# Gathering 32-row blocks as two transfers of 64 partitions, and building their plain form on TensorE

## The chip, the cores and the metric

The kernel runs on one core of a Trainium2 chip. The metric is the device time of one execution in microseconds. TensorE is called PE below, ScalarE ACT, VectorE DVE, GpSimd POOL and SyncE SP; SP, POOL and ACT also issue DMA transfers.

## The reference

One inference step of a two-layer trunk, for a prompt of 512 tokens and for 8 samples of 4 tokens each, which share the weights. Layer 0 mixes tokens with a gated DeltaNet, layer 1 with sliding-window attention; a SwiGLU block follows each. The change lies in the DeltaNet. Cut to what matters, with 16 heads of width 128 (the kernel works in chunks of 128 rows, the reference in chunks of 64; the recurrence is the same):

```python
kb = k * beta[..., None]
Bm = where(strict, einsum('bhncd,bhnsd->bhncs', kb, k) * decay, 0.0)
M = -Bm
T = eye(C) + M                       # T becomes inverse(I + Bm)
for _ in range(1, ...):
    Mp = Mp @ Mp
    T = T + T @ Mp
u = einsum('bhncs,bhnse->bhnce', T, v * beta[..., None])
...
def step(S, xs):                     # over the chunks, in sequence
    unew = uc - einsum('bhcd,bhde->bhce', wc, S)
    o = einsum(..., qc * exp(Gc), S) + einsum(..., ac, unew)
    S = S * exp(Gl) + einsum('bhcd,bhce->bhde', kc * exp(Gl - Gc), unew)
```

Each head's triangular matrix I + Bm is inverted chunk by chunk, and the state S then runs through the chunks.

## The kernel before

The Tile framework orders the instructions; the program order that it starts from is a string, PLAN (line 37). The 16 heads are four groups of four heads, g = 0 to 3, and the sequence is four chunks of 128. The steps of a group:

- t (tphase, lines 598 to 772): Gram matrices and decays on PE, ACT and DVE give `ba`, the 128x128 triangular blocks of 4 heads and 4 chunks, in two halves of two chunks.
- The inverse of the sixteen 32x32 diagonal blocks of a head is made on POOL. The blocks are written to DRAM (tile D1, line 702) and gathered into Lb (line 720) with one block on each partition. There are 64 blocks; Lb holds them twice, on partitions 0 to 63 and 64 to 127, so that each copy solves 16 of the 32 columns. A loop of 31 steps (lines 727 to 733) subtracts products, two instructions a step: `subt` and `Tn`. DVE transposes the result into `Tt` (line 735).
- Both forms then go through DRAM (tile D2): Tn and Tt are written (lines 740 and 741); the plain form is read into TU (line 746), the transposed form into the diagonal blocks of `ba` (line 750).
- m (merge, lines 774 to 817): two rounds of small matmuls per half (`pw`, `py`, and again `pw` and `py` at 64x64) turn the 32x32 inverses into 128x128 ones.
- c (chain, lines 838 to 890): over the four chunks `pk`, `pq`, `pu` on PE, the copy `un` on ACT, then `pS` and the new S on DVE, and `po`.
- s (sample, from line 900): the same for the 8 samples; o (out, line 1014): normalise, transpose, gate.

Beside them run the projections as dense passes: `win` (q, k, v), `wz` (gate), and `wa`, `wb` (two of the three passes of w_out, `wo`). Each dense product is three matmuls, since operands are split in high and low parts; one line (159) issues them. They are what PE does while a group's steps wait. The operands of `wa` are loaded from DRAM by eight SP transfers (`ogl`, line 300).

Tiles are taken from rings by tag. `sub` has three buffers (Lb, Tn, the samples' `wk` and Ue); `un` and `Kd` have one each. In `un` live the chain's un, the samples' `up` and merge's W2, in `Kd` the chain's Kd and the samples' `kp`. An instruction that writes a new tile of a tag waits until the last reader of the old one is done. POOL, too, works in program order, and has other small work: copies around the convolution (lines 539 to 549), memsets, and the reciprocal roots `rk` and `ro` (line 214).

Of the kernel before, what the change touches and what calls it, by code (L numbers as in the profile page):

```python
# [9 lines left out]
F32 = mybir.dt.float32  # L10
# [5 lines left out]
P = 128  # L16
# [10 lines left out]
NCH = SEQ // P  # L27
# [48 lines left out]
def kernel(  # L76
# [178 lines left out]
    with ExitStack() as gctx:  # L255
# [40 lines left out]
        def w_out_first():  # L296
# [9 lines left out]
            w_out_pass(0, ops)  # L306

        ops, ss1 = gdn(gctx, tc, locals())
        w_out_pass(2, ops)

# [87 lines left out]
def gdn(ctx, tc, env):  # L398
    nc, PE, DVE, ACT, POOL = (env[k] for k in ("nc", "PE", "DVE", "ACT", "POOL"))
    tmp, bank, dense, halves = (env[k] for k in ("tmp", "bank", "dense", "halves"))  # L400
    pc, kc, ident, ones, hrhs, rsqrt_col = (env[k] for k in ("pc", "kc", "ident", "ones", "hrhs", "rsqrt_col"))
    fillers = env["fillers"]
    dpool, ogsc = env["dpool"], env["ogsc"]
# [21 lines left out]
    p2 = ctx.enter_context(tc.tile_pool(name="g2", bufs=2))  # L425

    def big(tag, name, bufs, dt=F32, rows=P):
        return p2.tile([rows, 1024], dt, tag=tag, name=name, bufs=bufs)
# [169 lines left out]
    def tphase(q):  # L598
        g, KQ, KQS = q.g, q.KQ, q.KQS
# [76 lines left out]
        D1 = dpool.tile([4, NCH, 4, 32, 32], F32, tag="D1", name=f"D1_{g}")  # L676
        for hf in range(2):
            ba = p2.tile([P, 2, 4, 2, P], F32, tag="BA", name=f"BA{g}_{hf}", bufs=4)
            q.BA.append(ba)
            for n2 in range(2):  # L680
                n = 2 * hf + n2
                gr = bank("t", f"gram{g}_{n}")
                for j in range(2):
                    PE.matmul(gr[:, j * 256:(j + 1) * 256], lhsT=KQ[j][:, n, 0, :],
                              rhs=KQ[j][:, n].rearrange("p a b -> p (a b)"), start=True, stop=True)
                for j in range(2):
                    pe = bank("t", f"pe{g}_{n}_{j}")
                    PE.matmul(pe, lhsT=sel[:, n:n + 1].to_broadcast([68, P]),
                              rhs=bd[:, 4 * j:4 * j + 4].rearrange("p a b -> p (a b)"), start=True, stop=False)
                    PE.matmul(pe.rearrange("p (i c) -> p i c", i=2), lhsT=identr,  # L690
                              rhs=maskp.unsqueeze(1).to_broadcast([P, 2, 256]), start=False, stop=True)
                    for i in range(2):
                        h = 2 * j + i
# [6 lines left out]
            for b in range(4):  # L700
                bs = slice(32 * b, 32 * b + 32)
# [7 lines left out]
                  start=True, stop=False)  # L709
# [7 lines left out]


        Lb = big("sub", f"Lb{g}", 3)
        nc.sync.dma_start(Lb, D1.rearrange("b n h s c -> (b n h) (s c)").unsqueeze(0).to_broadcast([2, 64, 1024]))  # L720
        Lb = Lb.rearrange("p (s c) -> p s c", s=32)
        TU = big("sub", f"Tn{g}", 3)
        Tn = TU[:, :512].rearrange("p (s c) -> p s c", s=32)
        POOL.memset(Tn, 0.0)
        for k in range(2):
            POOL.memset(TU[64 * k:64 * k + 64, 16 * k:512:33], 1.0)
        for j in range(31):
# [6 lines left out]
        Tt = Lb.rearrange("p s c -> p (s c)")[:, :512].rearrange("p (c s) -> p c s", s=32)  # L734
        DVE.tensor_copy(Tt, Tn.rearrange("p a b -> p b a"))

        D2 = dpool.tile([2, 4, NCH, 4, 32, 32], F32, tag="D2", name=f"D2_{g}")
        for k in range(2):
            ks = slice(64 * k, 64 * k + 64)
            nc.sync.dma_start(D2[0].rearrange("b n h s c -> (b n h) s c")[:, :, 16 * k:16 * k + 16], Tn[ks])  # L740
            nc.sync.dma_start(D2[1].rearrange("b n h (s k) c -> k (b n h) s c", k=2)[k], Tt[ks])
        TU = TU.rearrange("p (u c) -> p u c", c=64)
        POOL.memset(TU[0:32, :, 32:64], 0.0)
        for b in range(3):
            o = 32 if b == 1 else 0
            nc.sync.dma_start(TU[32 * b:32 * b + 32, :, o:o + 32], D2[0, b].rearrange("n h s c -> s (n h) c"))
        for hf in range(2):
            for b in range(4):
                bs = slice(32 * b, 32 * b + 32)
                nc.sync.dma_start(  # L750
                    q.BA[hf][bs, :, :, 0, bs].rearrange("p n h c -> p (n h) c"),
                    D2[1, b, 2 * hf:2 * hf + 2].rearrange("n h s c -> s (n h) c"),
                )


# [13 lines left out]
        DVE.tensor_tensor(MT, MT, ident, ALU.add)  # L769
        DVE.tensor_tensor(q.TTs, pm3[:, 0:P], MT, ALU.add)  # L770

        q.TU = TU

    def merge(q):

        g, TU = q.g, q.TU
        for hf in range(2):
            ba = q.BA[hf]
            us = [(n2, h, 8 * hf + 4 * n2 + h) for n2 in range(2) for h in range(4)]

            def plain(t):

                return t.rearrange("p (b k c) -> p b c k", k=2, c=16)

            W1 = p2.tile([P, 8, 32], F32, tag="E", name=f"W1{g}_{hf}", bufs=2)
            pw = bank("v", f"pw{g}_{hf}")
            for i, (n2, h, u_) in enumerate(us):
                c = slice(i * 32, i * 32 + 32)
                PE.matmul(pw[32:64, c], lhsT=ba[0:32, n2, h, 0, 32:64], rhs=plain(TU[0:32, u_, 0:32]), start=True, stop=True)
                PE.matmul(pw[96:128, c], lhsT=ba[64:96, n2, h, 0, 96:128], rhs=plain(TU[64:96, u_, 0:32]), start=True, stop=True)  # L790
            for r in (32, 96):
                ACT.mul(W1[r:r + 32].rearrange("p h c -> p (h c)"), pw[r:r + 32, 0:256], -1.0)
            py = bank("v", f"py{g}_{hf}")
            for i, (n2, h, u_) in enumerate(us):
                c = slice(i * 32, i * 32 + 32)
                PE.matmul(py[0:32, c], lhsT=W1[32:64, i, :], rhs=ba[32:64, n2, h, 0, 32:64], start=True, stop=True)
                PE.matmul(py[32:64, c], lhsT=ba[32:64, n2, h, 0, 32:64], rhs=W1[32:64, i, :], start=True, stop=True)
                PE.matmul(py[64:96, c], lhsT=W1[96:128, i, :], rhs=ba[96:128, n2, h, 0, 96:128], start=True, stop=True)

            def v8c(t):  # L800
                return t.rearrange("p (n h c) -> p n h c", n=2, h=4)

            ACT.copy(ba[0:32, :, :, 0, 32:64], v8c(py[0:32, 0:256]))
            ACT.copy(TU[32:64, 8 * hf:8 * hf + 8, 0:32].rearrange("p u (k c) -> p u c k", k=2),
                     py[32:64, 0:256].rearrange("p (u c k) -> p u c k", u=8, k=2))
            ACT.copy(ba[64:96, :, :, 0, 96:128], v8c(py[64:96, 0:256]))
            pw2 = bank("v", f"pw2{g}_{hf}")
            for i, (n2, h, u_) in enumerate(us):
                c = slice(i * 64, i * 64 + 64)
                PE.matmul(pw2[64:128, c], lhsT=ba[0:64, n2, h, 0, 64:128], rhs=plain(TU[0:64, u_, :]), start=True, stop=True)  # L810
            W2 = p2.tile([P, 8, 64], F32, tag="un", name=f"W2{g}_{hf}", bufs=1)
            ACT.mul(W2[64:128].rearrange("p h c -> p (h c)"), pw2[64:128, 0:512], -1.0)
            py2 = bank("v", f"py2{g}_{hf}")
            for i, (n2, h, u_) in enumerate(us):
                c = slice(i * 64, i * 64 + 64)
                PE.matmul(py2[0:64, c], lhsT=W2[64:128, i, :], rhs=ba[64:128, n2, h, 0, 64:128], start=True, stop=True)
            ACT.copy(ba[0:64, :, :, 0, 64:128], v8c(py2[0:64, 0:512]))
# [283 lines left out]


    steps = {"kq": proj_kq, "t": tphase, "v": proj_v, "p": states, "s": sample, "m": merge, "c": chain, "z": proj_z, "o": out}
    groups = {}
    for step in PLAN.split():
# [10 lines left out]
        else:  # L1116
            g = int(step[-1])
# [419 lines left out]
```

## Time and profile before

| | us |
|---|---|
| median of 3 runs | 1753.47 |
| lowest, highest | 1748.12, 1753.71 |
| profiled execution | 1754.97 |
| its span in the trace | 1753.2 |
| PE busy in the span | 1648.0 (94%) |
| DVE, ACT, POOL busy | 947.7, 754.0, 230.0 |

The profiled execution is 1.8 us longer than its span and 1.5 us above the median. The DeltaNet takes the stretch from the start to 721 us, where the first SwiGLU's `wg` begins; the last `wz` matmuls end at about 541 us. In rows of the trace the names are the program's without the buffer numbers: `D` is D1 or D2, `Tn` also TU. A busy PE row counts a matmul from start to modelled end, so lengths of neighbours overlap.

### The profile page before, as it was taken

What the parts mean: (1) busy time and instruction counts of PE and PEld (TensorE: products, weight loads), DVE (VectorE), ACT (ScalarE), POOL (GpSimd) and SP (SyncE); (2) the same over time, 40 slices, a digit from 0 to 9 for tenths busy, and PEclk for the clock granted to TensorE, in tenths of its full rate; (3) what the DMA queues carried; (4) which work ended last, traced back from release to release, by engine and by line L of the source; (5) the groups of instructions that cost most, each with busy time, mean ns of one, the idle gap of its engine ahead of it and who ended that gap; (6) DMA issues with size and microseconds to landing.
All of it is one profiled execution on the core that took longest, in us unless ns stands there. A gap on an engine that the chain in (4) does not pass through costs nothing.

```text
span 1753.2 us, 33971 instructions
## 1 busy us (share of the span) xinstructions
PE 1648.0 (94%) x13370; PEld 1577.9 (90%) x13370; DVE 947.7 (54%) x2071; ACT 754.0 (43%) x1822; POOL 230.0 (13%) x474
## 2 busy tenths in 40 slices
PE   7997996898897899999999999999999999999997
PEld 6996896897786798999999999998779999999997
DVE  7985485467465646654444433456566554454333
ACT  5864484474555445433333323245444332332221
POOL 2216118106402500100000000000000000000001
PEclk9998898999898899999999999999799999999999
DMA  6232431442443464622322333443112233223332
GB/s 233 85 82 65 126 100 51 112 138 62 102 155 109 112 195 140 214 89 86 91 90 85 91 87 92 125 138 86 43 43 73 85 91 89 87 87 90 90 88 85
DMA packets 138487, 179.31 MB, mean 102 GB/s; under 512 B 58600, under 2 KB 66840, under 8 KB 136280
## 3 DMA queue, kind: packets, MB, share of 16 engines
q1 hardware_dynamic: 131096, 155.95, 30.7%
q0 software_dynamic: 3104, 14.67, 2.3%
q10 hardware_dynamic: 4128, 6.53, 1.2%
q8 instruction: 105, 1.72, 0.4%
q14 instruction: 54, 0.44, 0.1%
HBM read 146.84 MB, written 25.02 MB: 98 GB/s over the span
## 4 chain that ended last, share of the span: by engine, by line
PE 77%; POOL 7%; DMA 7%; ACT 4%; DVE 3%; issue 2%; SPq 1%; POOLq 0%; ACTq 0%; DVEq 0%
PE wg_p L159 15%; PE wu_p L159 15%; PE wd_p L159 14%; PE win_p L159 5%; PE wo_p L159 5%; PE wqkv_p L159 4%; DMA Lb<-D 3%; PE wz_p L159 3%; POOL Tn L733 3%; PE wao_p L159 3%; POOL subt L731 3%; PE ps L1242 1%; PE po L1272 1%; PE ptp L1266 1%; PE wdl_p L372 1%
## 5 line engine op out<-in xcount | busy, mean ns | idle before, releaser
L159 PE MATMUL wu_p<-hl,wh_wu 128*128 128x256 f32 (+1 forms) x704 | 199.7, 288 | 0.0
L159 PE MATMUL wg_p<-hl,wh_wg 128*128 128x256 f32 (+1 forms) x704 | 199.7, 288 | 0.0
L159 PE MATMUL wg_p<-hh,wl_wg 128*128 128x256 f32 (+1 forms) x704 | 199.2, 287 | 0.0
L159 PE MATMUL wu_p<-hh,wl_wu 128*128 128x256 f32 (+1 forms) x704 | 199.1, 287 | 0.0
L159 PE MATMUL wg_p<-hh,wh_wg 128*128 128x256 f32 (+1 forms) x704 | 198.5, 288 | 0.3 <-DVE g L329 0.3
L159 PE MATMUL wu_p<-hh,wh_wu 128*128 128x256 f32 (+1 forms) x704 | 198.8, 288 | 0.0
L159 PE MATMUL wd_p<-al,wh_wd 128*128 128x256 f32 (+1 forms) x660 | 190.4, 289 | 0.0
L159 PE MATMUL wd_p<-ah,wl_wd 128*128 128x256 f32 (+1 forms) x660 | 190.1, 288 | 0.0
L159 PE MATMUL wd_p<-ah,wh_wd 128*128 128x256 f32 (+1 forms) x660 | 188.1, 285 | 0.0
L135 DVE TENSOR_TENSOR wl_wd<-wr_wd,wh_wd 128x512 fp32r<-128x512 f32 x90 | 58.3, 648 | 151.7 <-ACT wh_wd L133 150.6
L159 PE MATMUL win_p<-hh0n,wh_win 128*128 128x256 f32 (+1 forms) x448 | 134.3, 302 | 2.0 <-ACT pre L541 2.0
L159 PE MATMUL win_p<-hl0n,wh_win 128*128 128x256 f32 (+1 forms) x448 | 135.0, 303 | 0.7 <-DVE hl0n L278 0.7
L159 PEld LDWEIGHTS wg_p<-hh,wh_wg 128*128 128x128 f32 x704 | 132.3, 188 | 0.4 <-DVE g L329 0.4
L159 PEld LDWEIGHTS wg_p<-hh,wl_wg 128*128 128x128 f32 x704 | 132.6, 189 | 0.0
L159 PEld LDWEIGHTS wu_p<-hh,wl_wu 128*128 128x128 f32 x704 | 132.6, 189 | 0.0
L159 PE MATMUL win_p<-hh0n,wl_win 128*128 128x256 f32 (+1 forms) x448 | 132.4, 299 | 0.0
L159 PEld LDWEIGHTS wu_p<-hh,wh_wu 128*128 128x128 f32 x704 | 132.4, 188 | 0.0
L159 PEld LDWEIGHTS wg_p<-hl,wh_wg 128*128 128x128 f32 x704 | 132.4, 188 | 0.0
L159 PEld LDWEIGHTS wu_p<-hl,wh_wu 128*128 128x128 f32 x704 | 132.4, 188 | 0.0
L133 ACT CAST wh_wg<-wr_wg 128x512 fp32r<-128x512 f32 x88 | 54.7, 621 | 178.6 <-PE wu_p L159 130.8
L133 ACT CAST wh_wd<-wr_wd 128x512 fp32r<-128x512 f32 x90 | 52.8, 586 | 174.7 <-PE wd_p L159 153.8
L159 PEld LDWEIGHTS wd_p<-al,wh_wd 128*128 128x128 f32 x660 | 124.1, 188 | 0.0
(452 smaller groups left out, 4506.3 us busy)
## 6 DMA issues: line engine op xcount, KB each, us to landing
wr_wg<-in_w_gu SPq DMA_DIRECT2D x88, 256.0 KB
wr_wu<-in_w_gu SPq DMA_DIRECT2D x88, 256.0 KB
wr_wd<-in_w_dn SPq DMA_DIRECT2D x75, 256.0 KB
wr_win<-in_w_in SPq DMA_DIRECT2D x64, 256.0 KB
Sg<-in_sdelta SPq DMA_DIRECT2D x8, 1024.0 KB
wr_wz<-in_w_in SPq DMA_DIRECT2D x32, 256.0 KB
out_ss<-Sg POOLq DMA_DIRECT2D x8, 1024.0 KB, 5.4
wr_wo<-in_w_out SPq DMA_DIRECT2D x32, 256.0 KB
```

The source lines that it names most:

```text
L133: ACT.copy(hi[:, :n], raw[:, o:o + n])
L135: DVE.tensor_tensor(lo[:, :n], raw[:, o:o + n], hi[:, :n], ALU.subtract)
L159: PE.matmul(ps[f][:m, :hw(f)], lhsT=wt[:, sl], rhs=xt[:, hc(f)], start=(k0 + j == 0 and wi == 0), stop=(k0 + j == total - 1 and wi == 2),)
L372: PE.matmul(p, lhsT=wt[i][:, sl], rhs=xt[k][:, c], start=(k == 0 and wi == 0), stop=(k == KF - 1 and wi == 2))
L731: POOL.tensor_tensor(tv, Lb[:, j, j + 1:32].unsqueeze(2).to_broadcast([P, r_, w]), Tn[:, j, 0:w].unsqueeze(1).to_broadcast([P, r_, w]), AL ...
L733: POOL.tensor_tensor(Tn[:, j + 1:32, 0:w], Tn[:, j + 1:32, 0:w], tv, ALU.subtract)
L1242: PE.matmul(sl, lhsT=q[rows, c, n * P:(n + 1) * P], rhs=kl[rows, a, ks], start=False, stop=True)
L1266: PE.transpose(ptp[:, c * 256 + kb * P:c * 256 + (kb + 1) * P], s[:, c, n, kb * P:(kb + 1) * P], ident)
L1272: PE.matmul(po[rows, n * P:(n + 1) * P], lhsT=vt[:, n - 1 + kb, kv * 64:kv * 64 + 64], rhs=pT[:, c, kb * P:(kb + 1) * P], start=(kb == k0 ...
```

## The change

1. The gather into Lb is two transfers of 64x1024 from the same DRAM tile, in place of one transfer with a leading broadcast of two.
2. Tn is taken from the tag `un` (one buffer) in place of `sub` (three buffers), with 512 in place of 1024 columns.
3. Only the transposed form goes through D2: two writes in place of four per group, and the three reads into TU are gone. The eight reads into `ba` are issued by SP and ACT in turn.
4. merge builds TU itself, once per half, in the tag `un`: a memset on DVE, 24 matmuls of 32x32 by the identity (`pd`), one copy on ACT (96x8x32) and one on DVE. The copy of `py` into TU moves from ACT to DVE.
5. W2 is taken from the tag `Kd` in place of `un`.

```diff
         Lb = big("sub", f"Lb{g}", 3)
-        nc.sync.dma_start(Lb, D1.rearrange("b n h s c -> (b n h) (s c)").unsqueeze(0).to_broadcast([2, 64, 1024]))
+        for k in range(2):
+            nc.sync.dma_start(Lb[64 * k:64 * k + 64], D1.rearrange("b n h s c -> (b n h) (s c)"))
...
-        TU = big("sub", f"Tn{g}", 3)
-        Tn = TU[:, :512].rearrange("p (s c) -> p s c", s=32)
+        Tn = p2.tile([P, 512], F32, tag="un", name=f"Tn{g}", bufs=1)
...
-            nc.sync.dma_start(D2[0].rearrange("b n h s c -> (b n h) s c")[:, :, 16 * k:16 * k + 16], Tn[ks])
-            nc.sync.dma_start(D2[1].rearrange("b n h (s k) c -> k (b n h) s c", k=2)[k], Tt[ks])
-        TU = TU.rearrange("p (u c) -> p u c", c=64)
-        POOL.memset(TU[0:32, :, 32:64], 0.0)
-        for b in range(3):
-            o = 32 if b == 1 else 0
-            nc.sync.dma_start(TU[32 * b:32 * b + 32, :, o:o + 32], D2[0, b].rearrange("n h s c -> s (n h) c"))
+            nc.sync.dma_start(D2.rearrange("b n h (s k) c -> k (b n h) s c", k=2)[k], Tt[64 * k:64 * k + 64])
...
-                nc.sync.dma_start(
+                (nc.sync, nc.scalar)[b % 2].dma_start(
...
     def merge(q):
...
+            TU = p2.tile([P, 8, 64], F32, tag="un", name=f"TU{g}_{hf}", bufs=1)
+            DVE.memset(TU[0:32, :, 32:64], 0.0)
+            pd = bank("v", f"pd{g}_{hf}")
+            for n2, h, u_ in us:
+                for b in range(3):
+                    bs = slice(32 * b, 32 * b + 32)
+                    PE.matmul(pd[bs, u_ * 32:u_ * 32 + 32], lhsT=ba[bs, n2, h, 0, bs], rhs=ident[bs, bs], start=True, stop=True)
+            pd8 = pd[:, 0:256].rearrange("p (u c) -> p u c", c=32)
+            ACT.copy(TU[0:96, :, 0:32], pd8[0:96])
+            DVE.tensor_copy(TU[32:64, :, 32:64], pd8[32:64])
...
-            ACT.copy(TU[32:64, 8 * hf:8 * hf + 8, 0:32].rearrange("p u (k c) -> p u c k", k=2),
-                     py[32:64, 0:256].rearrange("p (u c k) -> p u c k", u=8, k=2))
+            DVE.tensor_copy(TU[32:64, :, 0:32], py[32:64, 0:256].rearrange("p (u c) -> p u c", u=8))
...
-            W2 = p2.tile([P, 8, 64], F32, tag="un", name=f"W2{g}_{hf}", bufs=1)
+            W2 = p2.tile([P, 8, 64], F32, tag="Kd", name=f"W2{g}_{hf}", bufs=1)
```

The framework orders both kernels anew, so instructions move far from the edited lines. In the rows below the first number of a tile's name is its group (D1_3, Lb3 and BA3 are group 3's; un2_0 is chunk 0 of group 2's chain).

The first place is SP's queue around the last gather, Lb3. Before, the loads of the w_out operands stand on both sides of it:

```order
L702 DMA D1_3_6321<-BA3_0_6322 32x8x32 x4
L128 DMA wr_wo0_1_0_0_7990<-in_w_out 128x512
L128 DMA wr_wo0_1_0_4_7992<-in_w_out 128x512
L300 DMA ogl0_7871<-ogsc_78 128x544
L128 DMA wr_wo0_2_0_0_8057<-in_w_out 128x512
L702 DMA D1_3_6321<-BA3_1_6369 32x8x32 x4
L300 DMA ogl1_7877<-ogsc_78 128x544
L300 DMA ogl2_7883<-ogsc_78 128x544
L720 DMA Lb3_6424<-D1_3_6321 128x1x1024
L128 DMA wr_wo0_2_0_4_8059<-in_w_out 128x512
L300 DMA ogl3_7889<-ogsc_78 128x544
L300 DMA ogl4_7895<-ogsc_78 128x544
L300 DMA ogl5_7901<-ogsc_78 128x544
L300 DMA ogl6_7907<-ogsc_78 128x544
```

In the changed kernel they stand behind group 3's whole round trip:

```order
L702 DMA D1_3_6480<-BA3_0_6481 32x8x32 x4
L702 DMA D1_3_6480<-BA3_1_6528 32x8x32 x4
L721 DMA Lb3_6583<-D1_3_6480 64x1024 x2
L741 DMA D2_3_6684<-Lb3_6583 1024x1x32 x2
L745 DMA BA3_0_6481<-D2_3_6684 32x8x32 x2
L745 DMA BA3_1_6528<-D2_3_6684 32x8x32 x2
L300 DMA ogl0_8083<-ogsc_78 128x544
L300 DMA ogl1_8089<-ogsc_78 128x544
```

What moved: ogl0 to ogl2 went from ahead of the gather to behind the D2 write, which reads the finished substitution, and behind SP's reads of D2; ogl3 and the others, which followed the gather directly, went behind them too.

The second place is PE around the second chunk of group 2's chain. Before, its matmuls lie between `wz` matmuls and Gram work of group 3:

```order
L159 MATMUL wz3_3_p1_7276<-hh0n_3_628,wl_wz3_3_0_0_7283 128x288
L832 MATMUL pv3_1_6040<-kon_70,y29_6032 128x128 x4
L881 MATMUL pS2_1_6607<-un2_1_6605,Kd2_1_6581 128x128 x3
L688 MATMUL pe3_3_1_6403<-bd3_6313,sel_185 128x512
L690 LDWEIGHTS identr_186
L690 MATMUL pe3_3_1_6403<-maskp_183,identr_186 128x512
L881 MATMUL pS2_1_6607<-un2_1_6605,Kd2_1_6581 128x128
L847 MATMUL po2_1_6616<-un2_1_6605,BA2_0_4595 128x128 x4
```

In the changed kernel the whole chain of group 2 follows the last matmuls of group 3's Gram work (pm33), with no `wz` matmul left:

```order
L754 MATMUL pm3_6697<-kon_70,MT3_6695 128x128
L758 MATMUL pm23_6701<-MT3_6695,Mn3_6699 128x128
L762 MATMUL pm33_6705<-M13_6703,Mn3_6699 128x128
L880 MATMUL pS2_0_6723<-un2_0_6721,Kd2_0_6711 128x128 x4
L846 MATMUL po2_0_6729<-un2_0_6721,BA2_0_4701 128x128 x4
L861 MATMUL pk2_1_6740<-S2_6710,KQ2_3376 128x256 x2
L868 MATMUL pq2_1_6747<-S2_6710,KQ2_3376 128x256 x2
L875 MATMUL pu2_1_6754<-Vb2_1_4089,BA2_0_4701 128x128 x4
```

What moved: pS2_0, the first that needs a tile of the tag `un` from this chain, went behind all of group 3's Gram work, and with it the rest of the chain.

The third place is ACT's queue at the same point, in the changed kernel:

```order
L756 COPY Mn3_6699<-pm3_6697 128x128
L877 COPY un2_0_6721<-pu2_0_6716 128x512
L857 ACTIVATE Kd2_1_6735<-Kt2_4605,ckd2_4676 128x128
L745 DMA BA3_0_6481<-D2_3_6684 32x8x32 x2
L745 DMA BA3_1_6528<-D2_3_6684 32x8x32 x2
L851 COPY KQ2_3376<-po2_0_6729 128x2x256
L857 ACTIVATE Kd2_1_6735<-Kt2_4605,ckd2_4676 128x128 x3
```

The copy un2_0 stands ahead of ACT's four reads of D2_3 (two per half of `ba`), and the rest of the chain's work on ACT behind them.

## Rows read from the trace of the kernel before

**Rows 1.** The page, the chain that ended last: share of the span by engine
```profile
PE 77%; POOL 7%; DMA 7%; ACT 4%; DVE 3%; issue 2%; SPq 1%; POOLq 0%; ACTq 0%; DVEq 0%
```

**Rows 2.** Windows: stretch, length, busy PE, PEld, DVE, ACT, POOL, clock, DMA, GB/s
```profile
130.00:541.00 411.00, 357.50 (x3175) 333.59 (x3175) 244.27 (x558) 231.63 (x693) 138.93 (x292) 0.91 0.35 101
541.00:600.00 59.00, 38.01 (x325) 34.68 (x323) 32.90 (x66) 25.36 (x83) 34.63 (x65) 0.83 0.41 109
600.00:683.00 83.00, 82.57 (x768) 78.16 (x769) 43.86 (x114) 38.74 (x108) 5.05 (x7) 0.98 0.63 184
```

**Rows 3.** Chain of waits around the gathers: start, length, what
```profile
130.00 14.08 DMA Lb<-D
...
538.90 2.69 DMA D<-BA
541.68 14.85 DMA Lb<-D
```

**Rows 4.** DMA view, 130 to 145 us, 40 slices: share in tenths, GB/s
```profile
DMA  7981039441111111135931778321111111111111
GB/s 218 341 266 38 22 131 235 158 175 76 55 44 66 44 55 55 44 98 202 371 126 55 137 218 339 98 55 66 60 33 44 55 55 44 60 49 44 49 49 38
```

**Rows 5.** Chain of waits at two other loads from DRAM
```profile
186.95 4.24 DMA Tn<-D
...
1135.12 5.59 DMA kh<-hik
```

**Rows 6.** Timeline of POOL: start, length, line, instruction, [idle before <-releaser]
```profile
166.89 1.83 POOL L214 TENSOR_TENSOR rk<-ssk,mhalf 128x9 f32<-128x9 f32 x1
...
291.16 3.61 POOL L214 TENSOR_TENSOR ro<-sso,mhalf 128x17 f32<-128x17 f32 x1
...
556.67 0.23 POOL L731 TENSOR_TENSOR subt<-Lb,Tn 128x31 f32<-128x31 f32 x1 [45.52 <-DMA Lb<-D]
...
578.46 4.18 POOL L214 TENSOR_TENSOR ro<-sso,mhalf 128x17 f32<-128x17 f32 x1
...
595.50 0.22 POOL L733 TENSOR_TENSOR Tn<-Tn,subt 128x16 f32<-128x16 f32 x1
```

**Rows 7.** Timeline of PE: four matmuls that begin after idle time
```profile
170.34 0.42 PE L662 MATMUL prr<-kon,RR 128*68 128x128 f32 x1 [12.87 <-DVE RR L660]
...
300.82 0.44 PE L1034 MATMUL pTs<-kon,Os 128*128 128x128 f32 x1 [9.09 <-ACT wh_wz L133]
...
421.91 0.58 PE L881 MATMUL pS<-un,Kd 128*128 128x128 f32 x1 [6.51 <-ACT un L878]
...
558.60 0.58 PE L159 MATMUL wo_p<-oh,wh_wo 128*128 128x256 f32 x1 [10.64 <-ACT oh L303]
```

**Rows 8.** Timeline of ACT: operand load of w_out, fourth step of group 2's chain
```profile
557.90 0.65 ACT L303 CAST oh<-ogl 128x544 fp32r<-128x544 f32 x1 [12.35 <-DMA ogl<-ogsc]
...
566.02 0.61 ACT L878 COPY un<-pu 128x512 f32<-128x512 f32 x1
```

**Rows 9.** Tile py, 190 to 215 us: ns min/median/max, first and last start
```profile
L796 PE MATMUL py<-BA,W x32: 191/191/212, 199.3 to 210.7; 32*32 32x32 f32 x32
```

**Rows 10.** Chain of waits, last step of group 3's chain
```profile
680.05 0.86 PE pk L862 x4
...
681.03 0.86 PE pq L869 x4
...
683.71 0.91 PE pu L876 x8
...
684.64 0.59 ACT un L878
...
685.28 1.17 PE pS L881 x8
...
686.48 1.13 DVE S L885 x4
```

More of the change, by code (lines that the diff above doesn't have):

```diff
@@ L719, in tphase @@
         Lb = big("sub", f"Lb{g}", 3)
-        nc.sync.dma_start(Lb, D1.rearrange("b n h s c -> (b n h) (s c)").unsqueeze(0).to_broadcast([2, 64, 1024]))
+        for k in range(2):
+            nc.sync.dma_start(Lb[64 * k:64 * k + 64], D1.rearrange("b n h s c -> (b n h) (s c)"))
         Lb = Lb.rearrange("p (s c) -> p s c", s=32)
-        TU = big("sub", f"Tn{g}", 3)
-        Tn = TU[:, :512].rearrange("p (s c) -> p s c", s=32)
+        Tn = p2.tile([P, 512], F32, tag="un", name=f"Tn{g}", bufs=1)
+        TU = Tn
+        Tn = Tn.rearrange("p (s c) -> p s c", s=32)
         POOL.memset(Tn, 0.0)
@@ L735, in tphase @@
         DVE.tensor_copy(Tt, Tn.rearrange("p a b -> p b a"))
-        D2 = dpool.tile([2, 4, NCH, 4, 32, 32], F32, tag="D2", name=f"D2_{g}")
+        D2 = dpool.tile([4, NCH, 4, 32, 32], F32, tag="D2", name=f"D2_{g}")
         for k in range(2):
-            ks = slice(64 * k, 64 * k + 64)
-            nc.sync.dma_start(D2[0].rearrange("b n h s c -> (b n h) s c")[:, :, 16 * k:16 * k + 16], Tn[ks])
-            nc.sync.dma_start(D2[1].rearrange("b n h (s k) c -> k (b n h) s c", k=2)[k], Tt[ks])
-        TU = TU.rearrange("p (u c) -> p u c", c=64)
-        POOL.memset(TU[0:32, :, 32:64], 0.0)
-        for b in range(3):
-            o = 32 if b == 1 else 0
-            nc.sync.dma_start(TU[32 * b:32 * b + 32, :, o:o + 32], D2[0, b].rearrange("n h s c -> s (n h) c"))
+            nc.sync.dma_start(D2.rearrange("b n h (s k) c -> k (b n h) s c", k=2)[k], Tt[64 * k:64 * k + 64])
         for hf in range(2):
@@ L749, in tphase @@
                 bs = slice(32 * b, 32 * b + 32)
-                nc.sync.dma_start(
+                (nc.sync, nc.scalar)[b % 2].dma_start(
                     q.BA[hf][bs, :, :, 0, bs].rearrange("p n h c -> p (n h) c"),
-                    D2[1, b, 2 * hf:2 * hf + 2].rearrange("n h s c -> s (n h) c"),
+                    D2[b, 2 * hf:2 * hf + 2].rearrange("n h s c -> s (n h) c"),
                 )
@@ L770, in tphase @@
         DVE.tensor_tensor(q.TTs, pm3[:, 0:P], MT, ALU.add)
-        q.TU = TU
     def merge(q):
-        g, TU = q.g, q.TU
+        g = q.g
         for hf in range(2):
             ba = q.BA[hf]
-            us = [(n2, h, 8 * hf + 4 * n2 + h) for n2 in range(2) for h in range(4)]
-            def plain(t):
-                return t.rearrange("p (b k c) -> p b c k", k=2, c=16)
+            us = [(n2, h, 4 * n2 + h) for n2 in range(2) for h in range(4)]
+            TU = p2.tile([P, 8, 64], F32, tag="un", name=f"TU{g}_{hf}", bufs=1)
[8 more added lines that the diff above has]
+            DVE.tensor_copy(TU[32:64, :, 32:64], pd8[32:64])
             W1 = p2.tile([P, 8, 32], F32, tag="E", name=f"W1{g}_{hf}", bufs=2)
@@ L788, in merge @@
                 c = slice(i * 32, i * 32 + 32)
-                PE.matmul(pw[32:64, c], lhsT=ba[0:32, n2, h, 0, 32:64], rhs=plain(TU[0:32, u_, 0:32]), start=True, stop=True)
-                PE.matmul(pw[96:128, c], lhsT=ba[64:96, n2, h, 0, 96:128], rhs=plain(TU[64:96, u_, 0:32]), start=True, stop=True)
+                PE.matmul(pw[32:64, c], lhsT=ba[0:32, n2, h, 0, 32:64], rhs=TU[0:32, u_, 0:32], start=True, stop=True)
+                PE.matmul(pw[96:128, c], lhsT=ba[64:96, n2, h, 0, 96:128], rhs=TU[64:96, u_, 0:32], start=True, stop=True)
             for r in (32, 96):
@@ L809, in merge @@
                 c = slice(i * 64, i * 64 + 64)
-                PE.matmul(pw2[64:128, c], lhsT=ba[0:64, n2, h, 0, 64:128], rhs=plain(TU[0:64, u_, :]), start=True, stop=True)
-            W2 = p2.tile([P, 8, 64], F32, tag="un", name=f"W2{g}_{hf}", bufs=1)
+                PE.matmul(pw2[64:128, c], lhsT=ba[0:64, n2, h, 0, 64:128], rhs=TU[0:64, u_, :], start=True, stop=True)
+            W2 = p2.tile([P, 8, 64], F32, tag="Kd", name=f"W2{g}_{hf}", bufs=1)
             ACT.mul(W2[64:128].rearrange("p h c -> p (h c)"), pw2[64:128, 0:512], -1.0)
```

## The prediction

> **What bounds the kernel now.** I read the page first. The chain that ended last is 77% PE, with 7% DMA and 7% POOL [rows 1]: PE sets the time except where the DeltaNet's round trips make it wait. The windows say where: of the 411 us from 130 to 541, PE is busy 357.5 and idle 53.5, at a clock of 0.91; from 541 to 600 it is idle 21.0 of 59, at 0.83; from 600 to 683 it is idle 0.4 [rows 2]. So the change can pay only before 600, and it can cost anywhere.
>
> The chain of waits names the gather: 14.08 us for group 0, 14.85 for group 3 [rows 3]; there are four in all, of like length. While Lb0 is fetched the engine share falls to one tenth, with 44 to 55 GB/s in most of the late slices [rows 4]. One tenth of 16 engines is about two. POOL waits for it before the first `subt` (45.52 us in group 3, with other waits before it in that time) [rows 6], and what is queued behind on POOL comes late: `rk` of group 1 lies inside group 0's substitution, and PE waits 12.87 for a product of it; `ro` of group 0 lies inside group 1's, 3.61 long, and PE's wait before pTs is 9.09; 6.51 are lost before a pS of group 1's chain [rows 6, 7]. These three are 28.5 of the 53.5.
>
> **The gather.** Neither of its new transfers has a leading broadcast. The trace has no load of 64 partitions by 1024; the nearest is kh, four transfers of 64 by 512, the same 512 KB in all, in 5.59; a smaller round trip took 4.24 [rows 5]. I take 4.5. The lower bound is 3.7, the last D1 write's 2.69 and a margin of one for the larger size, the upper one 14.85, if the split changes nothing [rows 3]. That is 9.6 off group 0, and about 10 off group 3.
>
> The Trainium skill ("DMA: Bandwidth & Descriptors", section "Rules for kernel authors") says that an outermost dimension smaller than 16 confines a transfer to as many engines as it has entries. The trace agrees: two entries, and a share of 0.1 [rows 4]. The same page ("Issuing engines are not separate DMA queues") says that transfers issued by several engines still share the 16 engines, so that issuing from ACT saves only issue time. By that the alternating reads into `ba` would bring nothing in transfer; no run here shows it yet.
>
> **Round trip and merge.** Per group two D2 writes and three TU reads go, and the POOL memset, with PE's wait for the TU load. What comes instead are 24 matmuls, an ACT copy and a DVE copy per half. A matmul of this shape takes 0.19 [rows 9]; if they pipeline behind dense work they cost nothing, if one follows the other 24 x 0.19 = 4.6. I take 2 per half, since merge is a chain of short steps and each copy in it adds one more; ten for the five halves that still lie ahead of the end of wz.
>
> **Shared tags.** This part costs most. Tn now lives in the one buffer of `un`. The substitution of a group can only start when the chain of the group before is over, and the next chain's first `un` copy waits until the substitution has been transposed. Before, the two ran beside each other. Dense passes have to cover each in turn. For groups 1 and 2 there is enough of `win` and `wz`; only the first two steps of group 1's chain now stand together without dense work, 2 x 5.5 = 11 idle. On the other hand POOL's small work stands ahead of the substitution or early in it, so that the three long waits above go, in the main.
>
> **Sum up to the last wz.** 411 us, less 26 us of PE work that now comes after it (three steps of group 2's chain at 4.7, which is pk, pq, pu, pS of [rows 10] and a po like them, 14; the second merge half and Gram work of group 3, 12). Idle 53.5 becomes 12: -41.5. The clock lost 0.09 x 411 = 37 at most; fewer stalls give back a quarter, -10. Merge +10, the chain's cluster +11. That is 354.5: the last wz ends at 485 where it ended at 541. The bounds are wide: with all idle time and all of the clock recovered, 446; with 20 less recovered than I take, 505.
>
> **From there to the end of group 2's chain.** Here nothing covers the substitution. The order shows all loads of `ogl` behind SP's reads of D2_3, and the chain of group 2 behind Gram 3: PE has neither `wo` nor the chain. From 485: second merge half and Gram 3, 18 (estimate: eight steps of about 1 for the half, ten for the Gram work); D1 write 2.7, gather 4.5, substitution 34 (group 3's took 38.8 up to the last step, with `ro` of 4.18 in it [rows 6]), transposition 1: 545. Then the chain of four steps: one step is 0.86 + 0.91 + 0.59 + 1.17 + 1.13 [rows 10], with the update of V like that of S, 1.13, and gaps 0.4: 6.2, so 25. ACT, which issues reads of D2_3 behind the first un copy, waits there for the D2 write: 4.3 (like the TU load's round trip [rows 5]). The clock, after 40 us without work, costs 4 (0.17 x 25, with the 0.83 of [rows 2]). The chain ends at 578, where it ended at 569: its fourth `un` copy began at 566.02 [rows 8], and 0.61, 1.17 and 1.13 follow.
>
> **From there on.** Before, 114 us to the last wo matmul at 683. In them were some 8 idle (most of the 21.0 lie ahead of 569, and 0.4 after 600 [rows 2]), none of which need remain; two and a half steps of group 3's chain, 11, move behind that matmul; merge 3 adds 4. So 99, and the last wo ends at 677. The order has three steps of group 3's chain behind it, where one stood: 3 x 6.2 = 18.6, to 695.5. Before, S was done at 686.48 + 1.13 = 687.6 [rows 10]. The difference is +8. It could be split otherwise: 42 us without cover in the substitution, 33 in the chain and 15 at the tail, against what stood idle before there, 21 [rows 2] with 10.64 for the wo operands [rows 7, 8], and 56 gained earlier, of which 26 is work only moved. After 721 nothing changes.
>
> I take +9, on the profiled execution's 1754.97: 1764. That execution is 1.5 above the median of the runs, which is within what a run differs from another.
>
> **Rivals.** (1) Faster. The stalls before the last wz go altogether and the clock comes back, so that wz ends at 460: then the uncovered part starts 25 us earlier, and the time is 1764 - 25 = 1739. For it speaks that PE needs only 357.5 - 26 + 10 = 341.5 of busy time there, and 37 of that is a low clock; against it, that substitution, merge and chain are now one serial loop per group. It decides from a last wz at 471 downward. (2) The gather stays at 14 us because two transfers of one queue run one after the other, each narrow: +10 in group 3, in the open, and +9 in group 0: 1783. Against it is kh's 5.59 [rows 5]. (3) The cover returns: un2_0's wait is short since the substitution of group 3 begins far earlier than I place it, so the 42 us are half covered: 1743. The order of PE, with Gram 3 directly ahead of pS2_0, speaks against it. (4) Costs and gains cancel: wz ends near 475, and the time stays within 5 us of before. (5) ACT in groups 0 to 2 also waits in its queue for the D2 write, 4.3 each time, with evictions of the dense passes behind it: three times, 1777.
>
> **Chances.** A measurement of this kernel can tell about 0.3% (5.3 us) from no change. The forecast, slower by 6 to 25, has 0.40; (2), (5) and slips of the same kind 0.18; no difference that can be measured 0.20; faster, by (1) or (3), 0.22. The likeliest case alone reaches from 1757 to 1780. The range reaches to (1) and (3) below and past (2) above: 1741 to 1794.
>
> **What will show it.** Lb's rows of two transfers at 4 to 6 us, the engine share well above a tenth: if they stay at 14, rival (2). No PE wait before prr near 12.87 or before pTs near 9.09. The last wz matmul at 470 to 500. Then the substitution of group 3 with PE idle beside it for some 40 us at a low clock, and un2_0 directly behind it: if PE is busy there, the forecast is wrong in its main cost. Two more chain steps behind the last `wo` of the second pass. And `wg` of the first SwiGLU at about 730 where it was 721.

## The result, and the profile after

The changed kernel takes 1776.6 us (median of 4 runs, 1774.7 to 1778.2) against 1753.6 for the kernel before: a ratio of 1.011, 95% interval 1.006 to 1.015. It is 23 us slower. The prediction said slower, 1764, from 1741 to 1794. The profiled execution has a span of 1776.4. All of the difference lies ahead of the first SwiGLU: its first `wg` matmul starts at 741.3 where it started at 717.8 (the 721 given ahead of the prediction is where the last `wo` matmul lies), and what follows takes as long as before.

From the page of the kernel after, the busy times of the engines and the chain that ended last:

```profile
PE 1662.1 (94%) x13754; PEld 1579.8 (89%) x13754; DVE 956.0 (54%) x2095; ACT 753.4 (42%) x1822; POOL 224.4 (13%) x470
...
PE 78%; POOL 6%; DMA 5%; ACT 4%; DVE 4%; issue 3%; SPq 1%; POOLq 0%; DVEq 0%; ACTq 0%
```

The share of DMA in that chain fell from 7% to 5%, and that of POOL from 7% to 6% [rows 1]. PE is busy 14.1 us longer (1662.1 against 1648.0). Neither row tells where the time went; the windows do. Their columns are those of [rows 2]:

```profile
130.00:502.00 372.00, 340.44 (x3260) 315.35 (x3259) 235.79 (x540) 208.13 (x622) 140.72 (x286) 0.92 0.36 106
502.00:509.00 7.00, 4.51 (x102) 3.56 (x101) 2.95 (x6) 4.42 (x11) 0.27 (x1) 0.87 0.23 76
509.00:536.00 27.00, 18.57 (x53) 10.49 (x52) 13.92 (x27) 10.06 (x26) 0.50 (x3) 0.50 0.16 30
536.00:565.00 29.00, 0.00 (x0) 0.00 (x0) 0.63 (x2) 0.12 (x1) 22.22 (x62) 0.50 0.00 1
565.00:580.00 15.00, 12.22 (x71) 10.66 (x71) 6.53 (x16) 10.12 (x38) 0.00 (x0) 0.88 0.39 73
610.00:697.00 87.00, 84.01 (x823) 79.02 (x822) 46.20 (x114) 32.35 (x80) 2.71 (x4) 0.96 0.59 185
```

The last `wz` matmul starts at 502.0 where it started at 538.1 (the 541 given ahead of the prediction is some 2 us late). Up to there PE is busy 340.4 us and idle 31.6, at nearly the same clock as before [rows 2]. Then, behind 7 us of merge and Gram work, come 27 us at a granted clock of 0.50, the lower of the two levels, in which PE is busy 18.6; then 29 us in which PE does nothing, DVE and ACT next to nothing, and only POOL works. Before, the stretch after the last `wz` had 21 idle us of 59 [rows 2].

What the change was made of does work. The chain of waits of the kernel after, at the first and the last gather:

```profile
131.89 4.14 DMA Lb<-D
...
530.54 1.64 DMA D<-BA
...
532.79 4.27 DMA Lb<-D
```

The gather takes 4.14 and 4.27 us where it took 14.08 and 14.85 [rows 3]. The DMA view of 131 to 140 us, in 40 slices, shows what changed; the gather is the stretch from the fourth slice to the twenty-second, with weight loads beside it:

```profile
DMA  5688874986997898699996100000000000009398
GB/s 55 127 291 337 293 235 157 208 218 255 310 310 164 273 309 209 128 255 219 182 228 237 37 0 0 0 0 0 0 0 0 0 0 0 0 18 182 146 328 337
```

The engine share is 6 to 9 tenths in all but one of these slices, at 128 to 337 GB/s, where it fell to 1 tenth at mostly 44 to 55 [rows 4]. The weight loads are in these numbers; under e4 below the last gather is shown with next to nothing beside it.

The two waits of PE that the prediction turned on, in the timeline of PE:

```profile
166.48 0.40 PE L662 MATMUL prr<-kon,RR 128*68 128x128 f32 x1 [7.11 <-DVE RR L660]
...
565.52 0.80 PE L880 MATMUL pS<-un,Kd 128*128 128x128 f32 x2 [29.81 <-ACT un L877]
```

The wait before prr fell from 12.87 to 7.11 [rows 7]. The first pS of group 2's chain waits 29.81 us for the un copy. The timeline of ACT shows what that copy waited for:

```profile
564.88 0.59 ACT L877 COPY un<-pu 128x512 f32<-128x512 f32 x1 [32.79 <-DVE Lb L737]
567.64 0.40 ACT L857 ACTIVATE Kd<-Kt,ckd 128x128 f32<-128x128 f32 x1 [2.17 <-PE pS L880]
568.55 1.83 ACTq L745 DMA_DIRECT2D BA<-D  x4
570.43 0.59 ACT L851 COPY KQ<-po 128x512 f32<-128x512 f32 x1 [2.39 <-DMA BA<-D]
```

ACT stands idle 32.79 us before the copy, which is released by `Lb L737`, the transposition that ends group 3's substitution and frees the tag `un`. Behind it ACT waits 2.17 for pS and 2.39 for the reads that it issues itself.

### The profile page after: what moved, and what is told of

Same layout as the page of the kernel before. It is cut to its first block, busy times and chain, and to the rows that moved or that the text cites. A ratio compares the mean times of both kernels' runs of the same rounds, so it can differ in the third digit from the quotient of the medians.

```text
span 1776.4 us, 34732 instructions
## 1 busy us (share of the span) xinstructions
PE 1662.1 (94%) x13754; PEld 1579.8 (89%) x13754; DVE 956.0 (54%) x2095; ACT 753.4 (42%) x1822; POOL 224.4 (13%) x470
## 3 DMA queue, kind: packets, MB, share of 16 engines
q1 hardware_dynamic: 104016, 153.59, 29.5%
## 4 chain that ended last, share of the span: by engine, by line
PE 78%; POOL 6%; DMA 5%; ACT 4%; DVE 4%; issue 3%; SPq 1%; POOLq 0%; DVEq 0%; ACTq 0%
PE wg_p L159 15%; PE wu_p L159 15%; PE wd_p L159 14%; PE win_p L159 7%; PE wo_p L159 4%; PE wqkv_p L159 4%; PE wao_p L159 3%; POOL Tn L735 3%; POOL subt L733 2%; PE wz_p L159 2%; PE ps L1241 1%; PE gram L684 1%; PE ptp L1265 1%; PE pS L880 1%; PE po L1271 1%
```

## The experiments

All ratios are to the kernel before, with runs on the same chip. The order of the table is that of the text.

| | median us | ratio | 95% interval |
|---|---|---|---|
| changed kernel | 1776.6 | 1.011 | 1.006 to 1.015 |
| e1: before, with the split gather alone | 1728.4 | 0.985 | 0.980 to 0.990 |
| e4: changed, with one gather | 1804.8 | 1.027 | 1.024 to 1.030 |
| e2: changed, Tn in the tag sub | 1745.3 | 0.994 | 0.992 to 0.997 |
| e3: changed, group 2's chain first | 1735.7 | 0.989 | 0.985 to 0.994 |
| e7: e1, group 2's chain first | 1731.3 | 0.987 | 0.985 to 0.990 |
| e6: e3, all reads issued by SP | 1736.5 | 0.990 | 0.988 to 0.992 |
| e5: plain form alone, no newly shared single buffer | 1742.7 | 0.993 | 0.991 to 0.996 |
| e8: e5 with its new steps twice | 1763.2 | 1.006 | 1.003 to 1.010 |

The theory: the gather pays, and the tag `un`, which group 3's substitution now shares with group 2's chain, costs more than it pays. The rivals: the gather was hidden anyway; the plain form on PE is what costs.

**e1, the gather alone.**

```diff
--- kernel before
-        nc.sync.dma_start(Lb, D1.rearrange("b n h s c -> (b n h) (s c)").unsqueeze(0).to_broadcast([2, 64, 1024]))
+        for k in range(2):
+            nc.sync.dma_start(Lb[64 * k:64 * k + 64], D1.rearrange("b n h s c -> (b n h) (s c)"))
```

> The kernel before with only the gather as two transfers of 64 partitions; nearly the same order on every engine. Theory (the shared tag un costs, the gather pays): the gather falls from 14 to about 4 in each group, group 0's PE wait of 12.87 before prr shrinks to 3 or 7, group 3's substitution starts 10 earlier; 15 to 30 us faster than before, about 1731. Rival (the gather is hidden anyway, and what it frees is spent on the next wait): within 5 us of before.

Measured: 1728.4, 27.7 less than before in the same runs. PE, ACT and POOL have the order of the kernel before up to the first `wo` matmul, and the last `wz` ahead of it starts 18.5 us earlier (519.6 against 538.1); behind it `wo` and chain work change places. So the slow gather costs some 1.5% of the kernel; e4, which keeps the order of the changed kernel, gives the same price. The gather of group 0 in its chain of waits, and the longest waits of PE from 125 to 760 us (for what, total us, times, longest):

```profile
131.83 4.39 DMA Lb<-D
```

```profile
PE pw L790 <- DMA Tn<-D: 12.9, 4, 4.4
PE pTs L1035 <- ACT wh_wz L133: 9.1, 1, 9.1
PE prr L662 <- DVE RR L660: 7.5, 1, 7.5
...
PE wo_p L159 <- ACT oh L303: 1.4, 2, 0.8
```

The wait before prr is 7.5 (12.87 before), that of the w_out operands 1.4 in all where one alone was 10.64 [rows 7]. The 9.1 before pTs is as it was: `ro` still lies inside group 1's substitution on POOL.

**e4, the change without the split.** The changed kernel with the old gather; the order on every engine is the same as with the new one.

```diff
--- changed kernel
-        for k in range(2):
-            nc.sync.dma_start(Lb[64 * k:64 * k + 64], D1.rearrange("b n h s c -> (b n h) (s c)"))
+        nc.sync.dma_start(Lb, D1.rearrange("b n h s c -> (b n h) (s c)").unsqueeze(0).to_broadcast([2, 64, 1024]))
```

> The changed kernel with the gather as one transfer with the leading broadcast of two; the order on every engine is that of the changed kernel. Theory: 10 us more in group 0 and 10 in group 3 where nothing covers it, some in groups 1 and 2: 1792 to 1805. Rival (the gather is covered): within 6 us of the changed kernel.

Measured: 1804.8, 28 more than the changed kernel, at the upper end of the theory. So the split is worth the same 28 us in both surroundings, and the rest of the change costs 49 (e4's 1804.8 against 1756.2 for the kernel before in the same runs). Group 3's gather in the chain of waits, and two waits of PE:

```profile
544.11 12.95 DMA Lb<-D
```

```profile
PE pS L879 <- ACT un L876: 41.0, 4, 37.8
PE prr L662 <- DVE RR L660: 11.3, 1, 11.3
```

The wait of pS for un is 41.0 in all (32.9 with the split, of which 29.81 is one wait). Here group 3's gather has the DMA engines nearly to itself. The DMA view, in 40 slices, of e4 from 544 to 557 us and of the changed kernel from 532 to 538:

```profile
DMA  0000120001111211111111111111111111111100
GB/s 0 0 0 0 25 25 0 25 25 50 50 25 50 76 50 50 63 63 50 50 50 50 50 50 50 50 50 63 63 50 50 50 50 50 50 50 50 50 25 0
```

```profile
DMA  0000000000990127999798995610020000000000
GB/s 0 0 0 0 0 0 0 0 0 0 246 191 0 55 109 328 437 437 273 164 273 191 246 273 109 137 27 0 0 55 0 0 0 0 0 0 0 0 0 0
```

The same 512 KB go at a share of 1 tenth and some 50 GB/s in e4, and at 5 to 9 tenths in most of their slices with the split. So the low share is the transfer's own, and no other load's.

**e2 and e3, two ways out of the shared tag.**

```diff
--- changed kernel (e2)
-        Tn = p2.tile([P, 512], F32, tag="un", name=f"Tn{g}", bufs=1)
-        TU = Tn
+        TU = big("sub", f"Tn{g}", 3)[:, :512]
+        Tn = TU
```

> The changed kernel with Tn back in the tag sub, so that group 3's substitution and group 2's chain share no buffer. Theory: the 29.8 us wait before pS of group 2's first step goes, ogl loads go ahead of the gather again, and the time falls by 30 to 40, to 1737 to 1747; the three chain steps behind the last wo remain. Rival (the plain form on PE and the steps that it adds to merge cost the time): the wait may go, but the time stays over 1765.

```diff
--- changed kernel (e3), PLAN
-        "c1 t2 z1 o1 kq3 s2 m2 v3 t3 c2 z2 p3 z3 o2 s3 m3 c3 wa wb o3")
+        "c1 t2 z1 o1 kq3 s2 m2 v3 c2 t3 z2 p3 z3 o2 s3 m3 c3 wa wb o3")
```

> The changed kernel with one word of PLAN moved: group 2's chain ahead of group 3's tphase (c2 t3 in place of t3 c2); tags as changed. Theory: group 2's chain no longer waits for group 3's substitution, which then runs beside wo; 20 to 40 faster than the changed kernel, 1737 to 1757, less than e2 since all four chain steps of group 3 come behind the last wo. Rival (the plain form on PE costs the time): over 1765.

Measured: e2 1745.3, e3 1735.7, just under the range expected for it; 31 and 41 below the changed kernel. (The medians are from two sets of runs; by the ratios it is 29 and 38.) Both remove the wait; both are below before. The waits of PE, of e2 and then of e3:

```profile
PE pTs L1033 <- DVE ksT L952: 8.6, 1, 8.6
PE pTs L1033 <- ACT wh_wz L133: 8.2, 1, 8.2
...
PE pS L880 <- ACT un L877: 5.3, 6, 1.8
```

```profile
PE pd L780 <- DMA BA<-D: 6.0, 4, 2.9
...
PE pS L880 <- ACT un L877: 3.0, 4, 1.0
```

pS waits 5.3 and 3.0 in all, from 32.9. That e3 keeps every tag of the change, and moves one word, shows that it is not sharing as such that costs but this one meeting: in PLAN, groups 1 and 2 had their substitution behind the preceding chain already (c0 t1, c1 t2), only group 3 had it ahead (t3 c2). I had expected e2 to be the faster one; its median is 10 higher, though the intervals overlap, and its pTs waits of 8.6 and 8.2 are the nearest reason. All ten traces fit it: the waits of the pTs matmuls that need `ro` sum to 12.6 to 22.0 us in the six kernels with Tn in `sub` (13.8 before, 12.6 in e1, 22.0 in e5) and to 5.4 to 5.7 in the four with Tn in `un` (e3's longest is 3.0). POOL makes that `ro` some 12 us into group 1's substitution in the changed kernel and some 25 us into it in the kernel before. So the shared tag gave something back as well; no run moves `ro` by itself.

**e7, the same word moved without the shared tag.** e1, with c2 t3 in PLAN as in e3.

> e1 with group 2's chain ahead of group 3's tphase in PLAN. Theory: in e1 the two share no single buffer, so their order in PLAN is free, and the time stays within 6 of e1's 1728. Rival (the chain first is better by itself, whatever the tags, and e3 gained by that): 8 or more faster than e1.

Measured: 1731.3, with an interval that overlaps e1's. Where the two steps share no single buffer, their order brings nothing that these runs can tell; e3's gain is the tag's.

**e6, who issues the reads.** e3 with the eight reads into `ba` all on SP:

```diff
--- e3
-                (nc.sync, nc.scalar)[b % 2].dma_start(
+                nc.sync.dma_start(
```

> e3 with all reads into ba issued by SP. If issuing from two engines shortens the reads (each half's four reads land earlier), this is 4 to 12 slower than e3 (1735.7), with longer waits of pd for the reads. If the transfers take the same 16 engines whoever issues them and ACT's issues only block ACT, it is within 4 of e3 or faster.

Measured: 1736.5 against 1735.7; the intervals overlap. PE's wait of pd for the reads, of e6 (e3's is above):

```profile
PE pd L780 <- DMA BA<-D: 6.3, 5, 2.3
```

6.3 us in all against 6.0. What ACT loses by issuing is in its own list of waits, of the changed kernel and then of e3:

```profile
ACT pre L541 <- DMA BA<-D: 10.1, 2, 6.2
```

```profile
ACT pre L541 <- DMA BA<-D: 9.1, 2, 5.6
```

Behind its reads of groups 0 and 1 ACT stands for 10.1 us in the changed kernel and 9.1 in e3; in e6 there is no such wait, and the time is the same. The two issuing engines bring nothing that these runs can tell, and ACT's wait costs nothing.

**e5, the plain form alone.** e2 with TU in `sub` too and W2 back in `un`, so that beside e1 the plain form on PE and the issue of the reads differ, and no tag of one buffer gets a new user (TU's two halves are two more tiles of `sub` per group):

```diff
--- e2
-            TU = p2.tile([P, 8, 64], F32, tag="un", name=f"TU{g}_{hf}", bufs=1)
+            TU = big("sub", f"TU{g}_{hf}", 3)[:, :512].rearrange("p (u c) -> p u c", c=64)
...
-            W2 = p2.tile([P, 8, 64], F32, tag="Kd", name=f"W2{g}_{hf}", bufs=1)
+            W2 = p2.tile([P, 8, 64], F32, tag="un", name=f"W2{g}_{hf}", bufs=1)
```

> e1 with the plain form made on PE as in the change, but no tile moved into a shared single buffer: Tn and TU in the tag sub, W2 in un as before; reads into ba by SP and ACT in turn. What it tells apart: the worth of the plain form by itself, against e1 (1728). Theory now (each half of merge gets pd, an ACT copy and a DVE copy in series, 4 to 5 us, and group 3's last chain steps come behind the last wo): 1735 to 1750. Rival (the plain form saves the second round trip, and only the tags cost): 1715 to 1728.

Measured: 1742.7, 14 more than e1. Without a newly shared single buffer, the plain form on PE is dearer than the second round trip that it replaces. What the two more tiles of `sub` add to that, no run tests. The new steps of one half of group 3's merge, in the timeline of e5 (PE, ACT, DVE, PE):

```profile
631.29 0.59 PEld L780 LDWEIGHTS pd<-kon,BA 32*32 32x32 f32 x48
...
632.05 0.37 ACT L782 COPY TU<-pd 96x256 f32<-96x256 f32 x1 [1.41 <-PE pd L780]
...
632.45 0.42 DVE L783 COPY TU<-pd 32x256 f32<-32x256 f32 x1 [1.09 <-ACT TU L782]
...
635.55 0.10 PEld L789 LDWEIGHTS pw<-TU,BA 32*32 32x32 f32 x1
```

From the first pd at 631.30 to the first pw at 635.55 there are 4.25 us, where the matmuls take 0.70 and the copies 0.37 and 0.42: the rest is waiting from engine to engine and, in the 2.7 us behind the DVE copy, chain and dense matmuls that PE's order has in between. Where it comes out is the chains. On ACT, in e1 and then in e5, the first `un` copies of the chains of groups 2 and 3, and the last one of group 3:

```profile
496.91 0.58 ACT L879 COPY un<-pu 128x512 f32<-128x512 f32 x1
...
624.28 0.58 ACT L879 COPY un<-pu 128x512 f32<-128x512 f32 x1
...
662.03 0.59 ACT L879 COPY un<-pu 128x512 f32<-128x512 f32 x1
```

```profile
520.42 0.58 ACT L877 COPY un<-pu 128x512 f32<-128x512 f32 x1
...
650.15 0.58 ACT L877 COPY un<-pu 128x512 f32<-128x512 f32 x1
...
676.21 0.57 ACT L877 COPY un<-pu 128x512 f32<-128x512 f32 x1
```

Group 2's chain begins 23.5 us later and group 3's 25.9, while the last `wz` starts at about the same time in both (519.6 and 518.5): the chains are pushed out of the cover of the dense passes, and three steps of group 3's stand behind the last `wo` of the second pass, as in the changed kernel, where e1 has one. These two steps more, 6.9 us each, are the 14: the last `un` copy comes 14.2 us later.

**e8, the new steps twice.** To tell these steps from the order that the framework made around them, e5 got them a second time in series:

```diff
--- e5
             ACT.copy(TU[0:96, :, 0:32], pd8[0:96])
             DVE.tensor_copy(TU[32:64, :, 32:64], pd8[32:64])
+            pd = bank("v", f"px{g}_{hf}")
+            for n2, h, u_ in us:
+                for b in range(3):
+                    bs = slice(32 * b, 32 * b + 32)
+                    PE.matmul(pd[bs, u_ * 32:u_ * 32 + 32], lhsT=ident[bs, bs], rhs=TU[bs, u_, 0:32], start=True, stop=True)
+            pd8 = pd[:, 0:256].rearrange("p (u c) -> p u c", c=32)
+            ACT.copy(TU[0:96, :, 0:32], pd8[0:96])
+            DVE.tensor_copy(TU[32:64, :, 32:64], pd8[32:64])
```

> e5 with the three new steps of each merge half done twice in series: from TU, 24 more matmuls by the identity give the same plain form again, which ACT and DVE copy into TU once more. What it tells apart: what the added chain costs where it stands. If these steps are on the path that sets the end (2 to 5 us per half, eight halves, not all covered by dense work): 8 to 25 slower than e5 (1742.7). If they are covered and e5 is slower than e1 only by the order that the framework chose: within 4 of e5.

Measured: 1763.2, 20.5 more than e5. The first `un` copies of the same two chains:

```profile
529.11 0.58 ACT L885 COPY un<-pu 128x512 f32<-128x512 f32 x1
...
670.29 0.58 ACT L885 COPY un<-pu 128x512 f32<-128x512 f32 x1
```

Another 8.7 and 20.1 us later. So these steps are on the path: having them once costs 14, net of the round trip that they replace, a second time 20.5 (1.3% by the ratios, which are from two sets of runs), or 1.8 and 2.6 us for each of the eight halves.

No version with the plain form on PE beat e1, which changes two lines and has the lowest median here; the intervals of e7, e3 and e6 overlap with its. e3, with the plain form and all the shared tags, is 7 above it, which these runs cannot tell from nothing.

## Why the prediction was right, and where its sizes were off

The direction and the main mechanism were right; the size was not: +9 was forecast and +23 measured, inside a range of 53 us.

**Right: the place and the mechanism.** The main cost is the substitution of group 3 with nothing beside it, and un2_0 directly behind it. Rival 3 (the wait is half covered) is ruled out by the 29.81; e2 and e3 take the wait away and the time with it.

**Right: the gather.** Forecast 4.5, measured 4.14 and 4.27; rival 2 is out. The Trainium skill's rule on narrow transfers ("DMA: Bandwidth & Descriptors", section "Rules for kernel authors") agrees with both sides of it: a share of 1 tenth with a leading 2 (e4), of 5 to 9 tenths without. The rule of the Trainium skill on issuing engines (the same page, section "Issuing engines are not separate DMA queues") agrees with e6. Rival 5 named 1777, almost the time measured, but that is chance: the stall that it describes is there (10.1 us on ACT), and e6 takes it away with no change in time, as far as e3 stands for the changed kernel.

The split is worth more than the 9.6 and 10 us of groups 0 and 3 that the sum gave it: 28 in e1 and in e4.

**Too small: idle time before the last `wz`.** The sum had it end at 485; it was 502, just past the 470 to 500 that the prediction named as its sign. The terms that failed are the clock and the idle time. "Fewer stalls give back a quarter, -10": next to nothing came back, the clock is 0.92 where it was 0.91. And "idle 53.5 becomes 12" with 11 for the chain's cluster makes 23; it was 31.6. Here two errors partly cancelled. The cluster's idle time did not come: around the first two steps of group 1's chain (`un` copies at 362.80 and 377.11) PE is idle 1.2 us from 360 to 395. But the long waits did not go in the main: 7.11 stayed before prr and 5.6 before pTs, and the reads into `ba` cost 4.1 before pd. Busy time came out as forecast but for the clock: 357.5 - 26 + 10 = 341.5, measured 340.4. Rival 1 (wz ends at 460) failed on the same two, the idle time and the clock.

**Too small: Gram 3.** Forecast 18 from the last `wz` to D1's last write, measured 28.5 (502 to the write at 530.54). The terms, about 1 for a step, name no row and no low clock, and this stretch was 27 us at 0.50: with only merge and Gram work, in steps that wait for ACT, PE's clock fell before the long wait began, not behind it. The same twelve Gram matmuls in the kernel after (502 to 540 us) and before (500 to 545), with the busy time and the mean ns of one:

```profile
L684 PE MATMUL gram<-KQ 128*128 128x256 f32 x12 | 6.2, 674 | 1.5 <-ACT E L696 1.5
```

```profile
L684 PE MATMUL gram<-KQ 128*128 128x256 f32 x12 | 3.2, 388 | 0.0
```

They took 674 ns at the low clock where they took 388 at the full one, beside `wz` work. The prediction gave the low clock 4, and only to the chain that follows.

**Too large: the substitution.** Forecast 34, measured 27.0 (537.23 to 564.22). That gave back 7 of the 27.5 above, by luck: the 34 came from a row in which POOL had other engines beside it. The last section shows the rows. The chain of group 2 then had its fourth un copy at 591.86 where it had it at 566.02 [rows 8]: +26, forecast +9.

**The tail** came as forecast: three steps of group 3's chain behind the last `wo` of the second pass, 6.9 us apart (6.2 in the sum).

**Merge.** The sum had 2 per half. By e8 a second set of the steps costs 2.6 per half on the time of the whole kernel, 20.5 in all, where the sum had 14 (10 and 4); by e5 the plain form costs 14 net of the round trip. The size was nearly right.

The parts, measured in order: the split -28 (e1), the plain form and the shared tags +7 (e3 against e1), group 3's substitution ahead of group 2's chain in the shared tag +41 (the changed kernel against e3). Their sum is +20; measured are +23, from two sets of runs. The plain form without the tags is +14 (e5); the shorter pTs waits of e3 would put it below e5, as it is, but the intervals of the two overlap.

## What to carry to other kernels

A buffer that two steps share is an order between them: before a tile moves to a ring of one, ask which of its users run beside each other now, and which comes first in program order; one word in the plan was worth some 40 us here. The leading broadcast of two showed in the DMA view as a share of 1 tenth, and undoing it by itself was the cheapest gain here. A round trip through memory that runs beside dense work can be cheaper, as it was here, than three small steps on three engines that stand in the path.

## What the runs showed of the hardware

POOL's substitution ran faster when the others stood still. Its 62 instructions for group 3 in the kernel after, and then in the kernel before (busy us, mean ns of one):

```profile
L735 POOL TENSOR_TENSOR Tn<-Tn,subt 128x126 f32<-128x126 f32 (+22 forms) x31 | 11.5, 371 | 2.4
L733 POOL TENSOR_TENSOR subt<-Lb,Tn 128x126 f32<-128x126 f32 (+22 forms) x31 | 10.7, 346 | 30.0 <-DMA Lb<-D 27.6
```

```profile
L733 POOL TENSOR_TENSOR Tn<-Tn,subt 128x126 f32<-128x126 f32 (+22 forms) x31 | 16.8, 541 | 2.4
L731 POOL TENSOR_TENSOR subt<-Lb,Tn 128x126 f32<-128x126 f32 (+22 forms) x31 | 12.7, 411 | 47.8 <-DMA Lb<-D 45.5
```

The same instructions took 371 and 346 ns in the kernel after, when DVE was busy 0.6 of 29 us, and 541 and 411 before, when DVE was busy 25.3 of the 39.1 us that the loop took; together 22.2 us against 29.5. The Trainium skill ("SBUF — State Buffer", section "SBUF: two separate sides") says that a DVE instruction with two SBUF inputs and a GpSimd instruction that reads SBUF use one port pair, which the first of them holds while the other waits. These rows agree with it, though no run here varied DVE's work alone, and PE and ACT stood still as well.
